# A Strassen product done by the same scheme once more inside: one of seven products in the second input phase

## The chip, the core and the metric

The kernel runs on one core of a Trainium2 chip. The metric is device time: 910.96 us is the median of 3 runs of the kernel before (910.4 to 911.87). One execution was profiled; its trace gives every instruction of TensorE (PE, with its weight loads as PEld), VectorE (DVE), ScalarE (ACT), GpSimd (POOL) and SyncE (SP), and every DMA.

## What is computed

The reference is one layer of a pooling mixer on x (1 x 4096 x 1024, float32):

```
normed = rms_norm(x, norm_w)
u, gate = split(normed @ in_w, 2)            # in_w: 1024 x 2048
pooled = trailing means of u over 2/4/8/16 frames (4 channel groups) - u
mixed  = pooled (group by group) @ group_w + group_b
y      = mixed * scale * silu(gate)
out    = rms_norm(x + y @ out_w, final_norm_w)
```

## The kernel before

The kernel is three phases of matrix products, in float32. Every operand is cut into a high part that TensorE takes exactly and a low part with the rest (`split`, lines 167 to 170: ScalarE copies the high part, L165, VectorE subtracts to get the low part, L159), and a product is three matmuls: high-high, high-low, low-high (`mm3`, L603).

Phase "a" works on half of the channels, phase "b" on the other half; both take 4 blocks of 1024 frames. Phase "o" is the output projection, 8 blocks of 512 frames. A block of any phase is a product of 2 x 2 quarters, done by the scheme of Strassen and Winograd: 7 products P1 to P7 instead of 8, on sums of quarters. On the side of the frames the sums are S1 = A21 + A22, S2 = S1 - A11, S3 = A11 - A21, S4 = A12 - S2 in their usual names. In the input phases the order is P1, P2, P7, P6, P5, P4, P3; P3 is S4 times the weight quarter B22. One product is one step of the loop over `steps` (lines 1069 to 1071), so there are 28 + 28 + 56 steps.

A step of the input phases is 48 matmuls of 512 columns (`product_in`, line 609). P1 and P2 accumulate in PSUM banks 0 to 3; ScalarE copies P1's result to banks 4 to 7 as well, where P6, P5 and P3 are added on; P7 and P4 accumulate in banks 0 to 3. `evict_in` (line 806) takes the results out: ScalarE copies those of P1, P2, P6, P7 and P3, VectorE adds those of P5 and P4 onto earlier ones (L156). So while P3 runs in banks 4 to 7, banks 0 to 3 hold nothing that is still to be accumulated.

Operands come through 11 + 8 buffers of 128 x 1024 (`st` and `vt`, a queue by age: the one free the longest is taken). In phase a, `form_in` (line 547) normalizes the quarters of x and makes the sums; the operands of P1, P2, P7 and P4 are stored to DRAM by GpSimd's queue (`split_halves`, line 509), and phase b loads these four (`load_saved`, line 528) and makes S2 (for P6), S1 (for P5) and S4 (for P3) again with six subtractions and additions per block on VectorE. Four operand tiles (`op`) are used in turn.

Beside the products VectorE has the pooling of every half block: `pool` (line 745) is a chain of shifted additions on 128 x 1024, then L783 and L788, and a store to DRAM (`yd`). It is put off by some steps after P4 and P3 (`pool_later`, line 1116). In the last block of phase b the weights of phase o are loaded and split (`load_w`), one product's weights after each step.

Phase o has steps of 24 matmuls of 512 columns (`product_out`, line 716). Its order is P1, P7, P6, P2, P5, P4, P3, and VectorE adds each result onto x (`evict_o`, L1033). P6, P5 and P3 accumulate one after the other in the same pair of banks, so P3 can start there only when P5's result has been added out. In its blocks 2 to 7, P2 is already done by the same scheme once more inside (`product_inner`, L701, 42 matmuls of 256 columns in place of 24 of 512; `add_inner`, L711).

The framework orders each engine's instructions when the kernel is built, by the order in which they are written and `issue_after` marks; on the chip every queue is worked off in that order.

```
    def pool_later(n):
        kind, b, i = steps[n]
        if i == P4:
            args = (b, 0 if kind == "a" else 1, 1, ev.pop("22"), ev.pop("21"))
            wait = int(b == 0) if kind == "a" else 1 if b < NB - 1 else 2
```

## Time and profile before

| what | value |
|---|---|
| median of 3 runs | 910.96 us |
| profiled execution: its own time, its span | 911.84 us, 909.7 us |
| PE busy, PEld busy | 900.6 us (99%), 790.1 us (87%) |
| DVE busy, ACT busy, POOL busy | 764.5 us (84%), 461.8 us (51%), 49.9 us (5%) |
| phase b in the trace | 324.59 to 614.89 us |
| phase o in the trace | from 614.89 us |

PE's busy time says that PE is never without work in the middle of the kernel; what the reader needs beside it is how far the other engines are ahead of PE at each step. That is seen in tables by step (a step of phase b is 10.37 us, one of phase o 5.18 us) and in the timeline of one engine. In the timeline an instruction is shown with its full duration, while the next of the same engine starts a little before its end; the distance of the starts is what a full queue pays. A timeline's columns are start, duration (of all where there are several), engine, line, operation, tiles, shapes, and in brackets the idle time before it.

### The profile page before, as it was taken

Reading aid. Unit: us, or ns where it says so; the run is one execution under the profiler, and the core shown is the slowest. Engines: PE = TensorE matmul, PEld = TensorE weight load, DVE = VectorE, ACT = ScalarE, POOL = GpSimd, SP = SyncE. Lnnn points to the kernel's source line nnn. Section 1 sums busy time; section 2 is a strip of 40 time slices with the busy share of each in tenths; the row PEclk is TensorE's granted clock in tenths of the full one; section 3 lists DMA queues with packets and bytes.
Section 4 is the critical chain, followed back from the end, with each engine's and each line's share of the span. In section 5 each row is a group of like instructions: output and inputs, shape, how many; then the busy total and the mean of one; then the engine's idle time right before and its main releaser. Section 6 shows DMA issues by size and latency. Waiting matters only on the chain.

```text
span 909.7 us, 11455 instructions
## 1 busy us (share of the span) xinstructions
PE 900.6 (99%) x4320; PEld 790.1 (87%) x4320; DVE 764.5 (84%) x909; ACT 461.8 (51%) x693; POOL 49.9 (5%) x124
## 2 busy tenths in 40 slices
PE   9999999999999999999999999999999999999997
PEld 7888888888888888888888888888888898888886
DVE  3889995985995997696798699699989878978886
ACT  7869547547446565355445545644424424335334
POOL 0020100100110000000000000000201001001000
PEclk9999999999999999999999999999999999999998
DMA  9977766577675454116616714636385464464332
GB/s 341 401 291 240 276 235 230 189 270 253 217 272 196 156 202 145 47 64 212 255 47 234 275 70 158 235 105 219 137 280 181 149 226 155 146 232 139 116 139 93
DMA packets 66807, 178.08 MB, mean 196 GB/s; under 512 B 6080, under 2 KB 23872, under 8 KB 66752
## 3 DMA queue, kind: packets, MB, share of 16 engines
q1 hardware_dynamic: 60176, 155.83, 48.8%
q0 software_dynamic: 5856, 20.46, 6.1%
q10 hardware_dynamic: 720, 1.06, 0.3%
q8 instruction: 34, 0.56, 0.2%
q14 instruction: 21, 0.17, 0.1%
HBM read 116.50 MB, written 60.83 MB: 195 GB/s over the span
## 4 chain that ended last, share of the span: by engine, by line
PE 91%; DMA 4%; DVE 3%; issue 1%; ACT 0%; SPq 0%; POOL 0%; DVEq 0%; ACTq 0%; POOLq 0%
PE bank L603 88%; PE bank L701 3%; DMA early<-in_wut 2%; DMA st<-in_x 1%; DMA vt<-yd 1%; DVE vt L1033 1%; PE bank L406 1%; DVE op L159 1%; DVE st L159 0%; DVE vt L916 0%; ACT st L943 0%; DVE vt L162 0%; DVE vt L711 0%; SPq L370 0%; DVE st L1033 0%
## 5 line engine op out<-in xcount | busy, mean ns | idle before, releaser
L603 PE MATMUL bank<-op,w 128*128 128x512 f32 x2688 | 580.9, 379 | 0.0
L603 PEld LDWEIGHTS bank<-op,w 128*128 128x128 f32 x2688 | 508.5, 189 | 71.8 <-ACT bank L165 0.4
L603 PE MATMUL bank<-w,op 128*128 128x512 f32 (+1 forms) x1212 | 262.2, 377 | 0.0
L603 PEld LDWEIGHTS bank<-w,op 128*128 128x128 f32 x1212 | 226.3, 189 | 30.7
L165 ACT ACTIVATE op<-st 128x1024 fp32r<-128x1024 f32 x129 | 134.7, 1053 | 142.2 <-PE bank L603 90.5
L159 DVE TENSOR_TENSOR op<-st,op 128x1024 fp32r<-128x1024 f32 x129 | 156.8, 1222 | 51.7 <-ACT op L165 51.3
L156 DVE TENSOR_TENSOR vt<-vt 128x1024 f32<-128x1024 f32 (+6 forms) x72 | 88.2, 1236 | 0.6
L159 DVE TENSOR_TENSOR op<-vt,op 128x1024 fp32r<-128x1024 f32 x43 | 52.5, 1222 | 19.8 <-ACT op L165 19.6
L165 ACT ACTIVATE vt<-bank 128x512 f32<-128x512 f32 x82 | 47.6, 593 | 41.4 <-PE bank L603 40.5
L165 ACT ACTIVATE op<-vt 128x1024 fp32r<-128x1024 f32 x43 | 45.1, 1053 | 39.3 <-PE bank L603 30.2
L159 DVE TENSOR_TENSOR st<-st,st 128x1024 f32<-128x1024 f32 (+1 forms) x43 | 47.0, 1111 | 2.3 <-ACT st L912 1.3
L165 ACT ACTIVATE bank<-bank 128x512 f32<-128x512 f32 x48 | 27.9, 581 | 32.9 <-PE bank L603 32.9
L1033 DVE TENSOR_TENSOR vt<-bank,vt 128x512 f32<-128x512 f32 (+1 forms) x55 | 37.1, 677 | 7.4 <-PE bank L603 7.0
L165 ACT ACTIVATE st<-bank 128x512 f32<-128x512 f32 x48 | 27.8, 593 | 28.7 <-PE bank L603 22.3
L207 POOL TENSOR_SCALAR oms<-oss 128x2 f32<-128x2 f32 x14 | 8.4, 601 | 565.5 <-ACT st L912 460.6
L159 DVE TENSOR_TENSOR w<-st,w 128x1024 fp32r<-128x1024 f32 x25 | 30.2, 1223 | 7.8 <-ACT w L165 7.8
L165 ACT ACTIVATE w<-st 128x1024 fp32r<-128x1024 f32 x25 | 26.0, 1052 | 14.2 <-PE bank L603 9.6
L788 DVE SCALAR_TENSOR_TENSOR st<-vt,colt,st 128x512 f32<-128x512 f32 x46 | 32.7, 752 | 0.1
L1033 DVE TENSOR_TENSOR st<-bank,st 128x512 f32<-128x512 f32 x42 | 28.8, 692 | 3.9 <-PE bank L603 3.7
L783 DVE SCALAR_TENSOR_TENSOR vt<-vt,vt 128x1024 f32<-128x1024 f32 x24 | 29.4, 1227 | 0.3
L916 DVE SCALAR_TENSOR_TENSOR vt<-vt,ors,st 128x1024 f32<-128x1024 f32 x18 | 22.5, 1282 | 7.9 <-POOL ors L225 7.9
L165 ACT ACTIVATE st<-st 128x1024 f32<-128x1024 f32 x16 | 16.9, 1059 | 21.8 <-DVE st L156 21.7
(132 smaller groups left out, 619.0 us busy)
## 6 DMA issues: line engine op xcount, KB each, us to landing
st<-in_x SPq DMA_DIRECT2D x30, 512.0 KB, 5.3
st<-in_xt SPq DMA_DIRECT2D x28, 512.0 KB, 5.6
sd<-st POOLq DMA_DIRECT2D x28, 512.0 KB, 4.6
vt<-in_x SPq DMA_DIRECT2D x27, 512.0 KB, 4.5
st<-sd SPq DMA_DIRECT2D x24, 512.0 KB, 4.2
yd<-st SPq DMA_DIRECT2D x23, 512.0 KB, 2.6
st<-yd SPq DMA_DIRECT2D x20, 512.0 KB, 4.6
out<-vt SPq DMA_DIRECT2D x18, 512.0 KB, 3.6
```

The source lines that it names most:

```text
L156: nc.vector.tensor_tensor(out=dst, in0=a, in1=b, op=ALU.add)
L159: return nc.vector.tensor_tensor(out=dst, in0=a, in1=b, op=ALU.subtract)
L165: return nc.scalar.activation(dst, src, func)
L207: (nc.vector if on_vector and not first else nc.gpsimd).tensor_scalar(out=ms, in0=ss, scalar1=1.0 / D, scalar2=EPS, op0=ALU.mult, op1=ALU.add)
L406: latest[0] = nc.tensor.matmul(ps, a[:, kk, 2 * j + t, :], maps, start=t + m == 0, stop=t == 1 and m == len(pairs) - 1,).ins
L603: latest[0] = nc.tensor.matmul(ps, a, b, start=start and n == 0, stop=stop and n == 2, skip_group_check=True).ins
L701: latest[0] = nc.tensor.matmul(ps, x1, x2, start=i in (P1, P7) and k + n == 0, stop=k == 1 and n == 2, skip_group_check=True,).ins
L783: nc.vector.scalar_tensor_tensor(out=s[:, :, at : at + H], in0=s[:, :, at : at + H], scalar=1.0 / win, in1=v[:, :, HIST:], op0=ALU.mult, o ...
L788: nc.vector.scalar_tensor_tensor(out=sg[:, j], in0=s[:, j, at : at + H], scalar=bias_c[2 * grp + j], in1=sg[:, j], op0=ALU.add, op1=ALU.mult,)
L916: nc.vector.scalar_tensor_tensor(out=us[j], in0=us[j], scalar=rs[:, j : j + 1], in1=fw[0], op0=ALU.mult, op1=ALU.mult,)
L1033: partial["added"] = nc.vector.tensor_tensor(out=dst, in0=src, in1=dst, op=ALU.add).ins
```

## The change

P3 of each block of phase b (S4 times B22) is done by the scheme of seven once more: quarters of the quarter, 7 products of 12 matmuls of 256 columns (84 in place of 48 of 512). The inner P2, P4 and P3 add straight into banks 4 to 7; the inner P1 and, by copies of it, P6 and P5, and P7, use banks 0 to 3, from where VectorE adds them onto the rows (`to_rows`). The inner sums of the weight are made once, in block 0 (`form_inner_in`), and kept in four of the `st` buffers, which are lent until the end of phase b. The inner sums of S4 are made in each block (`split_inner_in`) and split into two operand tiles (`split_sums`).

Phase a now stores the operands of all seven products, and phase b loads all seven instead of making S2, S1 and S4. Loads of phase b are issued 2 steps ahead instead of 3 (but for the first three of block 0), some of phase o's first block 2 or 3 instead of 4. The pooling of P4's half in blocks 0 to 2 of phase b is put off by two steps instead of one. `make_wo` comes one step earlier. The buffers that phase o keeps for its own inner product are set aside from block 0 on.

```diff
@@ sd (operands that are stored)
-            for i in (P1, P2, P7, P4)
+            for i in ORDER_IN
@@ load_in, form_in, split_in
+        if q:
+            s[i] = load_saved(b, i)
...
+        if q:
+            t = split_halves(s[i])
+            if i == P3:
+                t = split_inner_in(t, s[i])
+            for u in s.pop(i):
+                give(u)
+            return t
@@ new functions
+    def split_inner_in(ts, us):
+        (a11, a21), (a12, a22) = ([quarter(u, g) for g in range(2)] for u in us)
+        vs = [take("p (n k s a) -> p n k s a", n=2, k=2, s=2) for _ in range(2)]
+        (s4, s2), (s3, s1) = ([v[:, n] for n in range(2)] for v in vs)
+        sub(s3, a11, a21)
+        sub(s2, a22, s3)
+        sub(s4, a12, s2)
+        add(s1, s2, a11)
...
+    def split_sums(t, n):
+        v, products = t["sums"][n]
+        o = next_op("p (x n k s a) -> p x n k s a", x=2, n=2, k=2, s=2)
+        split(o, v)
...
+    def inner_in(t, sets, then):
+        y, (one, six, seven, five) = sets["y"], sets["v"]
...
+        def to_rows(bank, *places):
+            src = bank.rearrange("p (c a s) -> p c s a", c=2, s=2)
+            for g, n in places:
+                dst = rows[n][:, :, HIST:].rearrange("p c (s a) -> p c s a", s=2)
+                dst = dst[:, :, :, g * P : (g + 1) * P]
+                add(dst, src, dst)
+        go(P2)
+        go(P1)
+        copy(six, one)
+        go(P4)
+        for c in range(2):
+            from_y(c)
+        to_rows(one, (0, 0))
+        go(P3)
+        then()
+        go(P6)
+        copy(five, six)
+        for c in range(2, 4):
+            evicted[0] = from_y(c).ins
+        to_rows(six, (1, 0))
+        go(P7)
+        to_rows(seven, (1, 0), (1, 1))
+        go(P5)
+        to_rows(five, (0, 1), (1, 1))
@@ pool_later
-            wait = int(b == 0) if kind == "a" else 1 if b < NB - 1 else 2
+            wait = int(b == 0) if kind == "a" else 2
@@ load_reach
-        return 4 if kind == "o" else 3
+        if kind == "o":
+            return 2 if (b, i) == (0, P1) else 3 if b == 0 and i in (P7, P6, P2) else 4
+        return 2 if kind == "b" and (b or i not in (P1, P2, P7)) else 3
@@ main loop
-        if kind == "o" and b == 1 and len(kept) < 4 and not inner_w:
+        if kind == "o" and b < 2 and not inner_w and (b or i in (P5, P4, P3)):
...
-        advance("split", n, split_step, split_reach)
+        due = lambda: advance("split", n, split_step, split_reach)
+        inside = kind == "b" and i == P3
+        if inside:
+            for half in range(2):
+                split_sums(split_up[n], half)
+        else:
+            due()
+        if kind == "b" and b == 0 and i in in_stages:
+            with tc.issue_after(latest_split[0]), tc.issue_after(latest_copy[0]):
+                form_inner_in(in_stages.index(i))
...
-        run(n)
+        run(n, behind=due if inside else None)
+        if kind == "b" and b == NB - 1 and i == P3:
+            st.end()
...
-            if kind == "b" and b in (1, 2) and i == P5:
+            if kind == "b" and b in (1, 2) and i == P6:
                 make_wo(b - 1)
```

More of the change, by code (lines that the diff above doesn't have):

```diff
@@ L56, in keep, with lend, end @@
         return self.renew(self.free.popleft()[1])
+    def lend(self):
+        t = self.free.popleft()[1]
+        self.lent.append(self.index_of(t))
+        return self.renew(t)
+    def end(self):
+        for i in self.lent:
+            Slots.clock += 1
+            self.free.append((Slots.clock, self.revert(i)))
     def give(self, ap):
@@ L119, with index_of, revert @@
     st = Slots(sts)
+    def index_of(t):
+        return next(i for i, u in enumerate(sts) if u is t)
     def renew(t):
-        i = next(i for i, u in enumerate(sts) if u is t)
-        return mem.tile([P, D], F32R, tag=f"st{i}", name=f"inner{i}")
-    st.renew = renew
+        return mem.tile([P, D], F32R, tag=f"st{index_of(t)}", name=f"inner{index_of(t)}")
+    def revert(i):
+        sts[i] = mem.tile([P, D], F32, tag=f"st{i}", name=f"st{i}")
+        return sts[i]
+    st.index_of, st.renew, st.revert = index_of, renew, revert
     vt = Slots(
@@ new lines, in split_inner_in @@
+    def split_inner_in(ts, us):
[6 more added lines that the diff above has]
+        add(s1, s2, a11)
+        t = {
+            P1: [quarter(ts[0][:, x], 0) for x in range(2)],
+            P2: [quarter(ts[1][:, x], 0) for x in range(2)],
+            P4: [quarter(ts[1][:, x], 1) for x in range(2)],
+        }
+        t["sums"] = ((vs[0], (P3, P6)), (vs[1], (P7, P5)))
+        return t
```

112 lines of the change are left out of this document (82 added, 30 removed).

## The prediction

> **What bounds the kernel now.** I read the page's busy times first, then PE's waits, then PE's timeline for the rates, then tables by step around the places that the change touches, and at the end VectorE's timeline there. The page:
>
> ```profile
> PE 900.6 (99%) x4320; PEld 790.1 (87%) x4320; DVE 764.5 (84%) x909; ACT 461.8 (51%) x693; POOL 49.9 (5%) x124
> PE 91%; DMA 4%; DVE 3%; issue 1%; ACT 0%; SPq 0%; POOL 0%; DVEq 0%; ACTq 0%; POOLq 0%
> ```
>
> PE's waits in the whole kernel:
>
> ```profile
> PE bank L406 <- DMA early<-in_wut: 1.0, 3, 0.4
> PE bank L1135 <- PEq L1433: 0.8, 1, 0.8
> PE bank L406 <- DMA early<-in_group_w: 0.4, 1, 0.4
> PE bank L701 <- DVE vt L711: 0.3, 1, 0.3
> ```
>
> After the start PE waits once, for 0.3 us. So matmuls that go away are worth their full time, and each wait that comes in costs its full time. PE's timeline gives the rates:
>
> ```profile
> 47.41 567.64 PE L603 MATMUL bank<-op,w 128*128 128x512 f32 x2628
> 614.89 88.22 PE L603 MATMUL bank<-w,op 128*128 128x512 f32 x408
> 702.95 1.50 PE L701 MATMUL bank<-w,op 128*128 128x256 f32 x12
> 706.29 2.75 PE L603 MATMUL bank<-w,op 128*128 128x512 f32 x12
> ```
>
> A matmul of 512 columns takes 567.5 / 2628 = 0.216 us; the 30 of 256 columns between 702.95 and 706.29 take 0.111 each. Phase b ends at 614.89, which I call O; a step is 10.37 us before O and 5.18 after it.
>
> How far VectorE is ahead at that border is told by the steps of the end of phase b and the start of phase o (columns: window, its length, then busy time of PE, PEld, DVE, ACT, POOL, clock, DMA share, GB/s):
>
> ```profile
> 542.30:614.89 72.59, 72.59 (x339) 63.62 (x338) 64.17 (x63) 39.92 (x55) 0.00 (x0) 1.00 0.49 167
> 583.79:594.15 10.36, 10.36 (x49) 9.08 (x48) 6.54 (x8) 4.95 (x7) 0.00 (x0) 1.00 0.62 204
> 594.15:604.52 10.37, 10.37 (x49) 9.08 (x48) 10.37 (x12) 4.83 (x7) 0.00 (x0) 1.00 0.15 51
> 604.52:614.89 10.37, 10.37 (x50) 9.08 (x49) 10.37 (x12) 6.36 (x8) 0.00 (x0) 1.00 0.45 151
> 614.89:625.26 10.37, 10.37 (x50) 9.09 (x49) 10.37 (x12) 5.53 (x9) 0.00 (x0) 1.00 0.61 205
> 625.26:635.63 10.37, 10.37 (x50) 9.09 (x49) 10.37 (x13) 2.08 (x2) 0.00 (x0) 1.00 0.63 212
> 635.63:646.00 10.37, 10.37 (x50) 9.09 (x49) 10.37 (x13) 1.06 (x1) 0.00 (x0) 1.00 0.23 91
> ```
>
> The whole last block leaves VectorE 8.4 us idle, but from 594 to 646 it has no idle time at all: it is working off a queue, and PE is only just not waiting. How much spare that is, its timeline says:
>
> ```profile
> 567.64 2.36 DVE L159 TENSOR_TENSOR op<-st,op 128x1024 fp32r<-128x1024 f32 x2
> 590.06 1.23 DVE L159 TENSOR_TENSOR w<-st,w 128x1024 fp32r<-128x1024 f32 x1 [2.52 <-ACT w L165]
> 591.20 0.68 DVE L156 TENSOR_TENSOR vt<-bank,vt 128x512 f32<-128x512 f32 x1
> 592.93 1.28 DVE L156 TENSOR_TENSOR vt<-bank,vt 128x512 f32<-128x512 f32 x2
> 640.99 1.43 DVE L788 SCALAR_TENSOR_TENSOR vt<-vt,colt,vt 128x512 f32<-128x512 f32 x2
> 643.45 0.71 DVE L1033 TENSOR_TENSOR st<-bank,st 128x512 f32<-128x512 f32 x1
> ```
>
> At full queue (distance of starts) an operation on 128 x 1024 costs 1.14 us, one on 128 x 512 0.60, an L788 0.66. The row at 591.20 adds out the first bank of P5 in the last block; the row at 643.45 adds out the first bank of P5 in phase o's first block. Phase o's P3 accumulates in that bank next and is due six steps after O, at 614.89 + 31.1 = 646.0. The add ends at 643.45 + 0.71 = 644.16: 1.8 us spare. This is the tightest place near the change.
>
> **The change, part by part.**
>
> PE: 84 matmuls for 48 gives 48 x 0.216 - 84 x 0.111 = 10.37 - 9.35 = 1.02 us per block, 4.1 us in all. This is the whole gain, all of it before O. TensorE's operands have the same kind of strides as in L701, so I keep 0.111.
>
> VectorE, per block: six operations go (S2, S1, S4 on two halves, 6 x 1.14 = 6.8 us), in the steps of P7, P6 and P5. Into P3's step come four sums of S4's quarters (4 x 0.60), two low parts (2 x 1.14) and six adds from banks 0 to 3 (6 x 0.60): 8.3 us. Net 1.5 us, small, but moved from steps with room to the step of P3. The weight's inner sums, once in block 0, are 4 x 0.60 + 2 x 1.14 = 4.7 us, in the steps of P7, P6 and P5, which have room as P5's shows:
>
> ```profile
> 366.06:376.43 10.37, 10.37 (x50) 9.09 (x49) 4.91 (x6) 3.06 (x5) 0.00 (x0) 1.00 0.18 60
> ```
>
> ScalarE gets two more splits (about 2 us) and two bank copies (1.2 us) per block. It is 50% busy in phase b, but in P3's step the copy of inner P1 to P6's bank and of P6 to P5's stand in line between splits: inner P5 starts 8.0 us after P3's start, and the copies, each half of the 1.06 us of a 128 x 1024, end about then. From 0 to 0.3 us per block; I take 0.
>
> Pooling: P4's half moves from P3's step to the next block's P1. One half is 7 shifted additions, 2 L783 and 4 L788: 9 x 1.14 + 4 x 0.66 = 13 us. In blocks 0 to 2 this only moves. But the last block, which had one half left over from block 2, now has two, while its own two still go to phase o. So the last block gets 13 + 1.5 us more on VectorE and had 8.4 idle.
>
> The queue at the border. As the changed kernel is built, VectorE's list between the same two adds (P5's first bank in the last block, P5's first bank in phase o) holds all that it held before and in addition six adds of 128 x 512 from the inner banks, three of the sums, two operand splits and one L783: 9 x 0.60 + 3 x 1.14 = 8.8 us. The stretch took 644.16 - 591.20 = 53.0 and will take 61.7. The room: the first add can't start before P5's first bank is done, which is three groups of six matmuls before P5's end (3.9 us), then P4 10.37, P3 9.35, six steps of phase o 31.1: 54.7 us. So PE must wait 61.7 - 54.7 = 7.0 us in phase o, at P3 or in pieces before it. To this comes a late start. The first half of P5's new weights is loaded into a buffer that the second half of P6's frees:
>
> ```profile
> 588.97 1.06 ACT L165 ACTIVATE w<-st 128x1024 fp32r<-128x1024 f32 x1 [2.69 <-PE bank L603]
> ```
>
> ```profile
> st<-wod SPq DMA_DIRECT2D x15, 512.0 KB, 4.2
> ```
>
> P6's weights are free at P6's end, 30.1 us before O (P5, P4, and P3 at 9.35); copy 1.06, low part 1.14, load 4.2, copy 1.06, low part 1.14 make 8.6, and the list has that low part right before the first add: it starts at O - 21.5 and not at O - 23.6, 2.1 us late. The loads' wait stands on SyncE's queue, where the first loads of phase o are behind it; they have over 10 us. Together 9.1 us.
>
> After the wait. From that add to the operand split that P7 of the next block needs, the list holds 11.2 us (five of 128 x 512, two L788, six of 128 x 1024, one tiny); PE has P3 and P1 in between, 10.4 us. Another 0.8 us, unless PE is slow here, since the wait is long. What the clock does in such a wait the trace shows at its end:
>
> ```profile
> 902.00:903.00 1.00, 1.00 (x10) 0.82 (x8) 0.72 (x5) 1.00 (x4) 0.00 (x0) 1.00 0.40 154
> 904.00:905.00 1.00, 0.00 (x0) 0.00 (x0) 0.85 (x4) 0.63 (x3) 0.00 (x0) 1.00 0.55 213
> 905.00:906.00 1.00, 0.00 (x0) 0.00 (x0) 0.93 (x4) 0.66 (x1) 0.00 (x0) 0.55 1.00 383
> ```
>
> ```profile
> 0.78 3.45 PE L1135 MATMUL bank<-const-bfloat16-1.0 128*128 128x512 bf16 x8 [0.78 <-PEq L1433]
> ```
>
> The clock is halved 2 us after the last matmul, and the eight matmuls at the very start ran at 0.43 us each, twice the 0.216. I take 3.45 us at half speed after the wait: 1.7 us, with which PE arrives after the split, so that the 0.8 is inside it. [...]
>
> Stores and loads: 24 stores of 512 KB more on GpSimd's queue in phase a, 24 loads more on SyncE's in phase b, 12.6 MB each way.
>
> ```profile
> 34.30:324.59 290.29, 290.29 (x1349) 254.34 (x1348) 245.97 (x291) 174.09 (x270) 26.21 (x49) 1.00 0.68 241
> 324.59:614.89 290.30, 290.30 (x1347) 254.49 (x1346) 243.16 (x244) 143.50 (x206) 0.00 (x0) 1.00 0.45 158
> ```
>
> ```profile
> sd<-st POOLq DMA_DIRECT2D x28, 512.0 KB, 4.6
> st<-sd SPq DMA_DIRECT2D x24, 512.0 KB, 4.2
> ```
>
> That is 43 GB/s more on 241 and 158. A load issued two steps ahead has 20.7 us for 4.2, so the loads are covered. The stores hold their buffers 4.6 us longer; most are taken again steps later. One place is tight: in phase a's first block the changed list puts P6's results into the buffers that P5's operands leave, after their store.
>
> ```profile
> 64.69 2.36 DVE L156 TENSOR_TENSOR st<-early,st 128x1024 f32<-128x1024 f32 x2
> 74.48 0.57 ACT L165 ACTIVATE st<-bank 128x512 f32<-128x512 f32 x1
> ```
>
> ```profile
> 75.76:86.13 10.37, 10.37 (x50) 9.09 (x49) 8.87 (x14) 10.36 (x16) 0.54 (x1) 1.00 0.68 207
> ```
>
> ```profile
> wvd<-early POOLq DMA_DIRECT2D x4, 512.0 KB, 7.5
> ```
>
> These operands are ready at 65.9 and 67.0 and P6's first result is copied out at 74.48, with ScalarE full behind it. A store that lands as fast as most (4.6) is done at 71.6, one as slow as the stores of that time (7.5) at 74.5, and one that has to wait for three issues of about a us more at 77.5. From 0 to 3 us; I take 0.
>
> Sum, against the profiled execution's own 911.84: 911.84 - 4.1 + 9.1 + 1.7 = 918.5. The median of the runs is 0.88 below that execution, so **917.7 us**.
>
> **The rivals.**
>
> 1. *VectorE takes the load and PE never waits* (faster): then only the 4.1 us is left, 906.9. For it: VectorE is 84% busy, and the last block has 8.4 us idle. Against it: the idle time lies before the first of the two adds, and the overrun is after it. It is faster only if the stretch grows by less than about 5 us instead of 8.8 (spare 1.8, less 1.0 for the shorter P3, plus the 4.1).
> 2. *The bound alone*: the loads of weights come sooner, so the late start doesn't happen, and the clock holds; 911.84 - 4.1 + 7.0 - 0.88 = 913.9.
> 3. *The clock holds*, because the wait comes in several short pieces: 0.8 in place of 1.7, 916.8. For it: P6's split is behind the same queue, so part of the wait comes there. Against it: the last add of P5 has the largest delay. [...]
> 4. *Stores hold up phase a as well*: the 3 us above on top of the forecast, 920.7. The first block's last steps would show PE waiting for ScalarE's copies out of banks 4 to 7.
> 5. *No change that can be measured*: the scheme does its work and PE waits about the 4.1 us that it saves, because part of the 8.8 us stands in VectorE's idle times; 911.
>
> **How the numbers follow.** Forecast 0.42, rival 1 0.09, rival 2 0.16, rival 3 0.17, rival 4 0.10, rival 5 0.06. A measurement of this kernel can tell about 0.2%, 1.8 us. Slower: 0.42 + 0.16 + 0.17 + 0.10 = 0.85; same 0.06; faster 0.09. The range leaves out rivals 1 and 5 and goes from a little under rival 2 to over rival 4: 912.8 to 921.5.
>
> **What would show it.** P3's steps in phase b at 9.35 us with the 256-column rate of 0.111; PE gapless through phase b; VectorE without idle from P5 of the last block until phase o's second block; PE waits of 7 to 9 us on VectorE's add of P5's result in phase o's first block, some of it a step or two earlier at P6; the granted clock at 0.5 there; no further PE waits after the second block. It is wrong if VectorE's adds from the inner banks or its list are shorter than counted, if PE waits already inside P3's steps, or if the first block of phase a shows waits.

## The result and the profile after

The changed kernel takes 933.31 us (median of 6 runs, 931.7 to 935.44), the kernel before 911.53 (6 runs on the same chip, 910.4 to 912.41): a ratio of 1.0241, 95% interval 1.023 to 1.0252, so 2.4% slower. The prediction was slower, 917.7 with a range up to 921.5. The sign was right; the time missed by 15.6 us.

The profiled execution of the changed kernel is its slowest, 935.44 us with a span of 933.5. Its page, and PE's waits in the whole kernel:

```profile
PE 904.6 (97%) x4464; PEld 793.8 (85%) x4464; DVE 776.1 (83%) x939; ACT 473.4 (51%) x711; POOL 56.5 (6%) x148
PE 61%; DVE 18%; DMA 11%; ACT 5%; issue 4%; POOL 1%; SPq 0%; DVEq 0%; ACTq 0%; POOLq 0%
```

```profile
PE bank L628 <- DVE st L1171: 6.0, 1, 6.0
PE bank L628 <- ACT st L183: 5.5, 3, 3.7
PE bank L709 <- ACT bank L183: 5.1, 5, 1.4
PE bank L628 <- DVE op L177: 2.3, 2, 1.4
PE bank L839 <- DVE st L849: 1.3, 1, 1.3
```

Before, PE waited 0.3 us after the start. Now results of ScalarE and of VectorE are late, in five kinds of places. (Of the changed kernel's lines, L183 is `copy` on ScalarE, L177 and L174 `sub` and `add` on VectorE, L628 the matmul of 512 columns, L709 that of the new inner product, L1171 the adds of phase o's results, L839 and L849 phase o's inner product and its adds.) PE's timeline says where they lie:

```profile
77.64 1.56 PE L628 MATMUL bank<-op,w 128*128 128x512 f32 x6 [1.27 <-ACT st L183]
...
227.46 12.85 PE L628 MATMUL bank<-op,w 128*128 128x512 f32 x45 [3.71 <-ACT st L183]
...
477.65 1.60 PE L709 MATMUL bank<-op,inner 128*128 128x256 f32 x12 [1.40 <-ACT bank L183]
...
625.48 1.60 PE L709 MATMUL bank<-op,inner 128*128 128x256 f32 x12 [0.91 <-ACT bank L183]
...
639.27 21.47 PE L628 MATMUL bank<-w,op 128*128 128x512 f32 x98 [1.40 <-DVE op L177]
...
666.78 12.29 PE L628 MATMUL bank<-w,op 128*128 128x512 f32 x48 [6.04 <-DVE st L1171]
680.00 20.34 PE L628 MATMUL bank<-w,op 128*128 128x512 f32 x93 [0.93 <-DVE op L177]
...
733.30 0.94 PE L839 MATMUL bank<-inner,op 128*128 128x256 f32 x6 [1.33 <-DVE st L849]
```

All kernels here have the same phases, so the clearest account is the time from the first matmul of a phase to the first of the next (of phase o to its last matmul). It comes from the start times of the matmuls in each profiled execution; before it is about 291, 290 and 288 us for phases a, b and o. The table gives the differences to that, of all kernels that ran, with the medians of their runs (the kernel before beside them: 911.53 for the changed kernel, 910.9 to 911.2 for the others):

| kernel | phase a | phase b | phase o | median us | ratio, 95% interval |
|---|---|---|---|---|---|
| changed kernel | +9.2 | +2.8 | +11.8 | 933.31 | 1.023 to 1.0252 |
| e3_stores | +7.9 | 0.0 | -0.4 | 918.43 | 1.0066 to 1.0096 |
| e22_behind | +7.6 | 0.0 | +0.3 | 918.53 | 1.0065 to 1.0095 |
| e23_both | +4.7 | +1.0 | -0.3 | 915.59 | 1.0028 to 1.0056 |
| e6_t3_later | +4.1 | +3.7 | +12.9 | 932.6 | 1.0219 to 1.0259 |
| e7_plain | +8.9 | +0.9 | +6.4 | 924.97 | 1.0125 to 1.0169 |
| e9_plain_kept | +8.9 | +1.5 | +2.0 | 921.78 | 1.0102 to 1.0132 |
| e16_plain_keep | +8.5 | +1.1 | +2.1 | 923.09 | 1.012 to 1.0147 |
| e2_last_plain | +8.0 | +2.8 | +4.5 | 925.56 | 1.0145 to 1.0176 |
| e8_norm_later | +9.0 | +2.1 | +4.4 | 926.62 | 1.015 to 1.018 |
| e10_last_kept | +9.0 | +2.0 | +4.7 | 925.84 | 1.0119 to 1.0172 |
| e13_last_copy | +8.2 | +2.8 | +2.5 | 924.98 | 1.0133 to 1.0166 |
| e17_last_keep | +7.9 | +2.7 | +1.0 | 921.81 | 1.0104 to 1.0144 |
| e1_pool | +9.1 | +3.5 | +12.9 | 933.71 | 1.0223 to 1.0261 |
| e5_no_copies | +7.9 | +3.5 | +12.9 | 934.37 | 1.0235 to 1.0268 |
| e11_copy_first | +7.6 | +3.4 | +12.7 | 933.34 | 1.0227 to 1.026 |
| e18_keep | +7.4 | +2.2 | +10.1 | 932.58 | 1.022 to 1.0264 |
| e4_formed | +0.4 | +18.1 | +14.4 | 941.89 | 1.0323 to 1.0354 |
| e21_one | 0.0 | -1.0 | -0.2 | 910.66 | 0.9986 to 1.0004 |

The prediction in this form is 0, -4.1 and +10.8. So the miss lies in phase a (9.2 us) and phase b (6.9). Phase o is 1.0 us off in sum, but not part by part, as the section on the prediction says.

### The profile page after: what moved, and what is told of

It reads as the page before. It is cut to its first block, busy times and chain, and to the rows that moved or that the text cites. A ratio compares the mean times of both kernels' runs of the same rounds, so it can differ in the third digit from the quotient of the medians.

```text
span 933.5 us, 11935 instructions
## 1 busy us (share of the span) xinstructions
PE 904.6 (97%) x4464; PEld 793.8 (85%) x4464; DVE 776.1 (83%) x939; ACT 473.4 (51%) x711; POOL 56.5 (6%) x148
## 4 chain that ended last, share of the span: by engine, by line
PE 61%; DVE 18%; DMA 11%; ACT 5%; issue 4%; POOL 1%; SPq 0%; DVEq 0%; ACTq 0%; POOLq 0%
PE bank L628 57%; DVE vt L174 5%; DVE op L177 4%; PE bank L839 3%; DMA early<-in_wut 2%; DMA st<-wvd 2%; DMA st<-wod 1%; DVE st L177 1%; DMA st<-sd 1%; DMA wvd<-early 1%; DMA st<-in_x 1%; PE bank L709 1%; DVE vt L177 1%; ACT op L183 1%; DVE st L174 1%
## 5 line engine op out<-in xcount | busy, mean ns | idle before, releaser
L628 PE MATMUL bank<-op,w 128*128 128x512 f32 x2496 | 543.7, 381 | 5.5 <-ACT st L183 5.5
L628 PEld LDWEIGHTS bank<-op,w 128*128 128x128 f32 x2496 | 473.2, 190 | 74.4 <-ACT st L183 6.7
L628 PE MATMUL bank<-w,op 128*128 128x512 f32 (+1 forms) x1212 | 264.8, 379 | 8.4 <-DVE st L1171 6.0
L628 PEld LDWEIGHTS bank<-w,op 128*128 128x128 f32 x1212 | 226.9, 190 | 40.9 <-issue 6.4
L183 ACT ACTIVATE op<-st 128x1024 fp32r<-128x1024 f32 x127 | 132.3, 1052 | 106.6 <-PE bank L628 69.5
L177 DVE TENSOR_TENSOR op<-st,op 128x1024 fp32r<-128x1024 f32 x127 | 153.8, 1220 | 31.8 <-ACT op L183 31.3
L183 ACT ACTIVATE op<-vt 128x1024 fp32r<-128x1024 f32 x53 | 55.7, 1054 | 79.3 <-PE bank L628 39.0
L174 DVE TENSOR_TENSOR vt<-vt 128x1028 f32<-128x1028 f32 (+6 forms) x72 | 86.9, 1232 | 0.4
L177 DVE TENSOR_TENSOR op<-vt,op 128x1024 fp32r<-128x1024 f32 x53 | 64.6, 1219 | 25.3 <-ACT op L183 25.3
L183 ACT ACTIVATE vt<-bank 128x512 f32<-128x512 f32 x88 | 50.2, 593 | 31.8 <-PE bank L628 31.7
L183 ACT ACTIVATE bank<-bank 128x512 f32<-128x512 f32 x56 | 32.7, 584 | 36.0 <-PE bank L628 35.8
L1171 DVE TENSOR_TENSOR vt<-bank,vt 128x512 f32<-128x512 f32 (+1 forms) x57 | 38.4, 676 | 6.3 <-PE bank L628 6.1
L183 ACT ACTIVATE st<-bank 128x512 f32<-128x512 f32 x42 | 23.8, 594 | 37.2 <-PE bank L628 21.6
L174 DVE TENSOR_TENSOR vt<-bank,vt 128x512 f32<-128x512 f32 (+1 forms) x63 | 40.6, 679 | 1.0 <-ACT bank L183 0.5
L177 DVE TENSOR_TENSOR st<-st,st 128x1024 f32<-128x1024 f32 (+2 forms) x29 | 30.7, 1074 | 12.3 <-DMA st<-wvd 8.6
L177 DVE TENSOR_TENSOR w<-st,w 128x1024 fp32r<-128x1024 f32 x25 | 29.9, 1218 | 8.1 <-ACT w L183 8.1
L1171 DVE TENSOR_TENSOR st<-bank,st 128x512 f32<-128x512 f32 x40 | 27.2, 686 | 7.2 <-PE bank L628 7.0
L183 ACT ACTIVATE w<-st 128x1024 fp32r<-128x1024 f32 x25 | 25.9, 1053 | 10.7 <-DMA st<-wod 8.0
L535 POOL DMA_DIRECT2D sd<-st x42 | 22.5, 537 | 132.5 <-DVE tmp L180 40.4
L709 PE MATMUL bank<-op,inner 128*128 128x256 f32 x192 | 23.8, 278 | 5.1 <-ACT bank L183 5.1
```

The source lines that it names most:

```text
L174: nc.vector.tensor_tensor(out=dst, in0=a, in1=b, op=ALU.add)
L177: return nc.vector.tensor_tensor(out=dst, in0=a, in1=b, op=ALU.subtract)
L183: return nc.scalar.activation(dst, src, func)
L535: first_saves.append(nc.gpsimd.dma_start(out=saved[h], in_=u).ins)
L628: latest[0] = nc.tensor.matmul(ps, a, b, start=start and n == 0, stop=stop and n == 2, skip_group_check=True).ins
L709: latest[0] = nc.tensor.matmul(ps, x1, x2, start=i in (P1, P7) and ct + k + n == 0, stop=k == 1 and n == 2, skip_group_check=True,).ins
```

## Experiments on phase a: the stores

**e3_stores**: the kernel before, with all seven sums stored and nothing else.

```
-            for i in (P1, P2, P7, P4)
+            for i in ORDER_IN
```

> The kernel before with one change: all seven operand sums of each block are stored in phase a, so 24 stores of 512 KB come in; nothing is loaded that was not loaded, nothing else is touched. Theory (the stores collide with other transfers of phase a): PE waits for ScalarE's copies out of banks 4 to 7 in the first block (about 2.3 us) and, in the third block, where a difference of two weight quarters is made from loads (line 313 of the changed kernel), 3.7 us and the halved clock after it (2.9 us): 909.7 + 9 = about 919 for the span, some 920.5 for the time. Rival (the stores alone are covered, and the two places come from another part of the change): 911.5, no change. If only the first block's buffers matter: 914.

It takes 918.43 us, 7.4 more, where 9 were expected, and has PE's waits of the changed kernel in the same two places (from start to start of the matmuls 1.1 and 0.7 us more at 75 to 78 us, 4.2 at 222), none elsewhere. The stores alone make most of phase a's loss, 7.9 of 9.2 us in the profiled executions. Most of the rest I put down to the halved clock after the second wait: in the changed kernel it is 0.50 for 5.8 us from the first matmul after that wait on (227.46 to 233.2), which costs 2.9 us, and in e3_stores the 7.9 less these waits leaves 1.9 for it, an estimate. How they do it shows in the third block, where `save_t3` loads four weight quarters and makes two differences. DMA and engines in that step, before and in the changed kernel (columns as in the prediction's tables):

```profile
199.31:209.68 10.37, 10.37 (x50) 9.09 (x49) 7.03 (x7) 7.30 (x11) 0.00 (x0) 1.00 0.61 191
```

```profile
201.20:211.50 10.30, 10.30 (x49) 9.02 (x48) 6.81 (x6) 7.08 (x12) 2.14 (x4) 1.00 1.01 362
```

The DMA engines go from 61% to full. The four loads of `save_t3` (L295 before, L313 after), minimum, median and maximum from issue to landing:

```profile
DMA to landing us min/median/max: 3.6/4.1/4.6
```

```profile
DMA to landing us min/median/max: 5.0/7.4/9.8
```

The loads are links of a chain: load, difference, store, load into the buffer that this frees, second difference, and then ScalarE can copy P6's result into the buffers that the differences held. Before, the two differences started at 208.88 and 218.75, and ScalarE came out of the chain just in time:

```profile
208.88 1.22 DVE L159 TENSOR_TENSOR st<-st,st 128x1024 f32<-128x1024 f32 x1
...
218.75 1.23 DVE L159 TENSOR_TENSOR st<-st,st 128x1024 f32<-128x1024 f32 x1 [0.20 <-DMA st<-wvd]
```

```profile
220.05 2.07 ACT L165 ACTIVATE st<-bank 128x512 f32<-128x512 f32 x4 [2.77 <-DVE st L159]
```

Now the second difference waits for its load, the copy for the difference, and P5's matmuls for the copy:

```profile
215.66 1.23 DVE L177 TENSOR_TENSOR st<-st,st 128x1024 f32<-128x1024 f32 x1 [4.31 <-DMA st<-wvd]
...
225.50 1.23 DVE L177 TENSOR_TENSOR st<-st,st 128x1024 f32<-128x1024 f32 x1 [4.25 <-DMA st<-wvd]
```

```profile
226.81 2.06 ACT L183 ACTIVATE st<-bank 128x512 f32<-128x512 f32 x4 [7.14 <-DVE st L177]
```

From the first load's issue (202.3 before, 204.7 now) to the first difference it is 10.9 us now and was 6.5: 4.4 longer, since the slowest of the four loads, 9.8 us, is one of the two that this difference needs. From there to the second difference it is 9.8 us now and was 9.9, so the load in between costs nothing more. ScalarE had stood idle 2.77 us for that buffer before and stands 7.14 now, 4.4 longer as well. Before, the copy began at 220.05 and P5's step at 220.9, so the chain had less than a us to spare; now PE waits 3.71, and its clock is 0.50 from 226.4 to 233.2.

**e22_behind** and **e23_both** take up the first block. There the trace has another link than the prediction's: S2's two stores wait for VectorE at the head of GpSimd's queue (3.57 and 0.72 us of idle time before them), two stores of weights stand behind them, and ScalarE's copy into the weights' buffer waits for these. ScalarE's timeline in the changed kernel, with P6's first copy-out 2.5 us later than before (74.48):

```profile
71.89 1.06 ACT L183 ACTIVATE w<-early 128x1024 fp32r<-128x1024 f32 x1 [2.42 <-DMA wvd<-early]
...
77.02 0.58 ACT L183 ACTIVATE st<-bank 128x512 f32<-128x512 f32 x1
```

e22_behind puts S2's stores behind the weights' (on top of e3_stores); e23_both also makes `save_t3` a step later.

```
-        later = q == 0 and b == 0 and i in (P1, P2)
+        later = q == 0 and b == 0 and i in (P1, P2, P6)
# e23_both, too:
-        if kind == "a" and b == 2 and i == P7:
+        if kind == "a" and b == 2 and i == P6:
```

> The run with the stores alone (the kernel before, all seven sums stored), but in the first block S2's two stores stand behind the stores of weights on GpSimd's queue and not ahead of them. Theory (S2's stores wait for VectorE, the weights' stores stand behind them in order and land late, ScalarE's copy into the weights' buffer waits 2.4 us for that, and the copies out of P6's banks stand behind it): PE's waits of 1.1 and 0.7 us at 75 to 78 go; the one at 222 stays: 918.4 less 1.8 to 2.2, about 916.4. Rival (P6's results wait for a buffer that is still being stored, as the prediction had it, or for the traffic as a whole): the two waits stay, 918.

> The same, and in addition the difference of two weight quarters a step later (P6 of block 2), as in the run with that edit on the changed kernel. Theory (these are the two places where the stores cost): 911.2 and up to 1.5 more for what that edit left at 254 to 330 us in the changed kernel: 911 to 913. Rival (what is taken away in one place comes back in the next steps of phase a): 914 to 917.

In e22_behind the copy into the weights' buffer does not wait any more, and in its place the copy-out does, for the buffer that S1's store holds, as the prediction had bounded it:

```profile
75.41 0.60 ACT L165 ACTIVATE st<-bank 128x512 f32<-128x512 f32 x1 [1.50 <-DMA sd<-st]
```

The two waits fall from 1.8 us in e3_stores to 1.25, and the time does not change (918.53, the rival's 918 and not the theory's 916.4). Both links end within a us of each other; taking one away leaves the other. e23_both is 3 us better than the stores alone, and 4.6 above the kernel before: the wait at 222 is gone, and waits of 1.75, 1.27 and 0.9 us stand at 254, 266 and 329 us in its place. The theory's 911 to 913 was wrong here, the rival right.

**e6_t3_later** makes that last edit alone in the changed kernel.

> The changed kernel, but the difference of two weight quarters (lines 307 to 318: four loads, two subtractions, two stores) is made in block 2's step of P6 and not of P7, one step later. Theory (its loads collide with four stores of sums that are issued within 3 us before them, land in 7.4 us and not 4.1, and the buffers that the difference holds come back too late for P6's results): with the loads away from these stores PE's wait of 3.7 us and the halved clock after it go, 5.6 to 6.6 less: 927 to 928. Rival (the difference holds buffers wherever it stands while stores are under way): the wait moves a step or two later and stays, 931 to 935.

Median 932.6, 0.7 below the changed kernel and within its spread. The theory's 927 to 928 missed. Phase a is 5.1 us shorter in the profiled execution, of which 0.9 and 1.1 come back in phases b and o; the wait at 224 is gone, and shorter ones stand at 255, 267 and 329 us. So the long wait hangs on where these loads stand, and a place for them that costs nothing was not found. The edit moves the whole chain and not the landing alone; that the slow landing makes the wait rests on the chain's times above.

## Experiments on phase o: the border

**e2_last_plain** and **e1_pool** part two explanations of the wait at phase o's P3: the longer list on VectorE, or the second half of the pooling in the last block.

```
# e2_last_plain
-            if i == P3:
+            if i == P3 and b < NB - 1:
                 t = split_inner_in(t, s[i])
# e1_pool
-            wait = int(b == 0) if kind == "a" else 2
+            wait = int(b == 0) if kind == "a" else 1 if b < NB - 1 else 2
```

> The changed kernel, but the last block's P3 in phase b is a plain product of 48 matmuls, as in the kernel before; blocks 0 to 2 keep the scheme. Theory (VectorE's queue between the two adds of P5's first bank decides): that list falls from 61.0 to 52.3 us, which it was before, so PE's waits at P3 of phase b's last block (1.7), at the second and sixth step of phase o (1.4 and 6.0), the halved clock (1.7) and the wait after it (0.9) go: 11.7 less and 1.0 more for the plain product, 922 to 924. Rival (the load of the last block as a whole, with two halves of the pooling in it, or the late start of the weights decides): the waits at the border shrink by 2 to 5 us only, 929 to 932.

> The changed kernel, but P4's half of the pooling stands where it stood before (one step after P4 in blocks 0 to 2), so the last block of phase b has one half less of it, 13 us of VectorE. Theory (the list between the two adds decides): that list is 59.9 instead of 61.0 us, so PE's waits at the border shrink by about 1 us, while the pooling back in P3's step may cost ScalarE's bank copies 0 to 2 us: 931 to 935. Rival (the second half of the pooling overloads the last block): the border's 11.7 us go, 921 to 924.

e1_pool takes 13 us of VectorE out of the last block and changes nothing (933.71; the wait at P3 is 6.8 us). In e2_last_plain the two adds of the prediction (P5's first bank in the last block and in phase o's first) start 52.3 us apart and not 62.3, and the waits at phase o's third step and at its P3 are gone (the second and the sixth in the expectation, which counts from 0). Phase o falls from +11.8 to +4.5. The time, 925.56, lies between the theory's 922 to 924 and the rival's 929 to 932, since one wait of 3.07 us is left, with which phase o still loses 4.5:

```profile
670.92 1.35 PE L628 MATMUL bank<-w,op 128*128 128x512 f32 x4 [3.07 <-DVE op L177]
```

**e7_plain**, the changed kernel with a plain P3 in all blocks, has that wait too (4.1 us at 666), so it is not the scheme's. It takes 924.97, the rival's 921 or more and not the theory's 918 to 919. Its VectorE timeline there (L1050 is the norm's product):

> The changed kernel without its inner scheme: all seven sums are stored and loaded, and P3 of phase b is a plain product of 48 matmuls in all four blocks. Theory (stores cost phase a 7.4 us; the loads cost nothing; without the scheme VectorE has 6.8 us less in each block than before, the list between the two adds is 48.5 us, and PE waits nowhere from phase b on): 911.0 + 7.4, 918 to 919, with no wait of PE after 230 us. Rival (loads of sums two steps ahead, or the moved half of the pooling, cost something by themselves in phase b or at the border): 921 or more.

```profile
662.88 1.23 DVE L177 TENSOR_TENSOR st<-vt,vt 128x1024 f32<-128x1024 f32 x1 [2.52 <-issue]
...
666.82 2.48 DVE L1050 SCALAR_TENSOR_TENSOR st<-st,ors,st 128x1024 f32<-128x1024 f32 x2 [0.92 <-POOL ors L243]
669.22 1.22 DVE L177 TENSOR_TENSOR op<-st,op 128x1024 fp32r<-128x1024 f32 x1
```

The first row makes S3 for P7 of phase o's second block. In the built list its target is the buffer whose pooled result went off to DRAM at 658.59; it starts 4.3 us later, after 2.52 us in which VectorE stands idle. That it waits there for this store to land is my reading; stores from `st` to `yd` take 3.6 us in the median of the changed kernel. Then a final norm's chain (square, root, reciprocal, two products) stands in the list, and only behind it the split that P7 waits for. In the kernel before, S3 went to another buffer and did not wait, and the split stood ahead of the norm's products. Three runs look for the edit that did this.

**e8_norm_later** calls that norm a step later (with the last block plain). **e9_plain_kept** (all plain) and **e10_last_kept** (last block plain) undo one edit of the diff, which sets four buffers aside already in phase o's first block:

```
# e8_norm_later, in evict_o
-        elif not final and i in (P4, P3):
+        elif b and not final and i in (P4, P3):
             finish(b, 1 if i == P4 else 0)
+        elif not b and i == P3:
+            with tc.issue_after(latest_split[0]):
+                finish(b, 1)
+            finish(b, 0)
# e9_plain_kept, e10_last_kept
-        if kind == "o" and b < 2 and not inner_w and (b or i in (P5, P4, P3)):
+        if kind == "o" and b == 1 and not inner_w:
```

> As the run with a plain P3 in the last block, and in addition the first half of phase o's first final norm (called at line 1240 in P4's step) is called a step later, behind the split of P7's operand, so that this split stands ahead of the norm's two products in VectorE's list. Theory (what was left of the border's wait, 3.2 us and the halved clock after it, is VectorE waiting in order for the norm's square, root and reciprocal with that split behind): 925.6 less 5, 920 to 921. Rival (the split is late because VectorE has more to do, not because it waits): 1.7 us less at most (its two idle times there), 924.

> As the run with a plain P3 in all four blocks, and in addition the four buffers for phase o's inner weights are set aside when they were before (in phase o's block 1 and not already from P5 of block 0). Theory (with four buffers fewer at the border, the sum for P7's operand is written to the buffer whose pooled result is just being stored, and has to wait 2.5 us for that store to land, with the final norm's chain ahead of the split; with the buffers free the sum gets one that has long been idle): PE's wait of 4.2 us and the halved clock after it go, 925.0 less 6, 918 to 919.5, which is the kernel before plus the stores' 7.4. Rival (the wait comes from the later loads or the moved pooling): 924 to 926.

> As the run with a plain P3 in the last block, and in addition the four buffers for phase o's inner weights are set aside when they were before. Theory (as in the run with plain P3 and this edit, and nothing else is late): PE's wait of 3.2 us at P7 of phase o's second block and the halved clock after it go, 925.6 less 5 to 6, 919.5 to 920.5. Rival (VectorE is behind after the border in any case, as the run with the norm a step later showed, where the wait moved to phase o's third block): the wait moves to 710 to 740 us and stays, 924 to 927.

The wait at 666 to 670 is gone in all three, so either change takes it away, the norm's place in the list or the buffers. But in all three a wait of 2.5 us comes in at 716 to 718, in phase o's third block, behind the next norm (e9_plain_kept 921.78, e8_norm_later 926.62, e10_last_kept 925.84), and no theory's time was met (e10_last_kept fell within its rival's). **e16_plain_keep** (all plain), **e17_last_keep** (last block plain) and **e18_keep** (scheme in all blocks) undo a second edit besides, the number of spare buffers in phase o:

```
-        elif kind == "o" and b:
+        elif kept:
             keep[0] = 0
```

> The changed kernel with a plain P3 in all blocks, with the four buffers set aside as before, and in addition the spare of three vt buffers is dropped in phase o only while buffers are set aside (as before) and not in every block from 1 on. Theory (the way in which buffers are shared out orders VectorE's list so that operand splits stand behind the norm's chain; with both edits undone they do not): the wait of 2.5 us at 715.7 goes, 921.8 less 2.6, 919 (the kernel before plus the stores' 7.4). Rival (the moved pooling or the loads): 921 to 922.

> The changed kernel with a plain P3 in the last block alone, and both edits of the buffers undone. Theory (with the last block plain the list between the two adds is as before, and with the buffers as before nothing else is late after phase b): no wait of PE after 600 us, 925.8 less 5 to 6, 919.5 to 920.5; what stays above the kernel before is the stores (7.4) and the waits in P3's steps (3.9) less 3.05. Rival (VectorE's total work at the border): a wait of 2 to 4 us stays after 640 us, 923 to 926.

> The changed kernel with both edits of the buffers undone and the inner scheme in all four blocks. Theory (the list between the two adds, 61 against 52 us, makes the wait of 6 us at phase o's P3 and the halved clock, the buffers make the small waits after it): the wait at P3 stays, those after it (0.9 and 1.3) go: 933.3 less 2.2, 931. Rival (the buffers make the large wait too): under 927.

Now PE's waits in e17_last_keep, and in e18_keep:

```profile
PE bank L628 <- ACT st L183: 5.4, 3, 4.0
PE bank L709 <- ACT bank L183: 4.4, 4, 1.4
...
PE bank L839 <- DVE vt L849: 0.8, 1, 0.8
```

```profile
PE bank L628 <- DVE st L1171: 6.0, 1, 6.0
...
PE bank L628 <- DVE op L177: 1.5, 1, 1.5
...
PE bank L839 <- DVE vt L849: 0.8, 1, 0.8
```

With the last block plain and the buffers as before, phase o loses 1.0 us; with the scheme in the last block it loses 10.1, and the wait of 6.0 at P3 is there as in the changed kernel. So of phase o's 11.8 us the list makes 9.1 (e18_keep less e17_last_keep) or 7.3 (the changed kernel less e2_last_plain), and the buffers 1.7 (the changed kernel less e18_keep) or 3.5 (e2_last_plain less e17_last_keep), since the two causes overlap. e18_keep, at 932.58, is near its theory's 931; e17_last_keep, at 921.81, has lost the large waits after 600 us, and lies above its theory's 919.5 to 920.5 since its phase b is +2.7. The small rest of 1.0 us (waits of 0.8 to 0.9 at the inner products) was not followed: e16_plain_keep, where 919 was expected, has two of them and takes 923.09, which is no better than e9_plain_kept.

## Experiments on phase b: the inner products

In P3's steps PE waits for the copies from bank to bank. ScalarE's timeline in block 1 shows why they are late: the line is full from 471.7 to 478.6, and the copy of P6's bank (476.97) stands behind two splits of the next product and four copies out.

```profile
471.69 1.07 ACT L183 ACTIVATE st<-st 128x1024 f32<-128x1024 f32 x1 [1.12 <-DVE st L174]
472.66 0.59 ACT L183 ACTIVATE bank<-bank 128x512 f32<-128x512 f32 x1
473.17 1.05 ACT L183 ACTIVATE op<-st 128x1024 fp32r<-128x1024 f32 x1
474.11 1.08 ACT L183 ACTIVATE vt<-bank 128x512 f32<-128x512 f32 x2
475.07 1.07 ACT L183 ACTIVATE op<-st 128x1024 fp32r<-128x1024 f32 x1
476.02 1.09 ACT L183 ACTIVATE vt<-bank 128x512 f32<-128x512 f32 x2
476.97 0.63 ACT L183 ACTIVATE bank<-bank 128x512 f32<-128x512 f32 x1
477.49 1.08 ACT L183 ACTIVATE op<-vt 128x1024 fp32r<-128x1024 f32 x1
```

**e5_no_copies** leaves the two copies out (its sums lack P1 in P6's bank and P6 in P5's); **e11_copy_first** puts the second ahead; **e13_last_copy** has that order, a plain last block and the buffers set aside later.

```
# e5_no_copies
-        copy(six, one)
-        copy(five, six)
-                            ps, x1, x2, start=i in (P1, P7) and ct + k + n == 0,
+                            ps, x1, x2, start=i in (P1, P7, P6, P5) and ct + k + n == 0,
# e11_copy_first
-        then()
         go(P6)
-        copy(five, six)
-        for c in range(2, 4):
-            evicted[0] = from_y(c).ins
+        with tc.issue_after(copy(five, six).ins):
+            for c in range(2, 4):
+                evicted[0] = from_y(c).ins
+            then()
```

> The changed kernel without the two copies from bank to bank in each inner P3: inner P6 and P5 start their banks afresh, so the sums of P1 with P6 and of P6 with P5 are left out of the result. Theory (the copies stand in ScalarE's line behind splits and copies out, and PE waits for them; in the last block that wait is part of the border's and comes back there): PE's waits in P3's steps go in blocks 1 and 2, 3.4 to 4.3 us less, 929 to 930. Rival a (the waits are those of the banks that the copies read, not of the copies): no change, 933. Rival b (all five waits count in full): 6 us less, 927.

> The changed kernel, but in inner_in the copy of P6's bank to P5's is put ahead of the copies out of banks 6 and 7 and of the next step's splits on ScalarE. Theory (ScalarE's order alone makes this copy 2 us late, PE waits 1.4 us for it in blocks 1 and 2): these two waits go and no other takes their place; the last block's comes back at the border: 933.3 less 2.8, 930 to 931. Rival (the splits, now later, make the next block's P1 wait, or VectorE is behind there anyway): 932.5 to 935.

> Three of the edits together: plain P3 in the last block, the buffers set aside later, and the copy from P6's bank ahead in ScalarE's line. If each names its wait rightly, only the stores' 7.4 us and the first copy's wait (0.6 to 0.8 in blocks 1 and 2) are left beside the three blocks' gain of 3.05: 911.2 + 7.4 - 3.05 + 1.4 = 917. Rival (the waits are of VectorE's total work and move on when one is taken away): 922 to 926.

e5_no_copies takes 934.37, and the theory's 929 to 930 missed. The waits for copies are gone, in block 1 without any other in their place; in block 2's P3 step PE waits 1.4 us for VectorE's add, and in the last block there are others.

```profile
540.08 1.60 PE L709 MATMUL bank<-op,w 128*128 128x256 f32 x12 [1.41 <-DVE st L174]
```

e11_copy_first takes 933.34: no wait for the second copy, but 0.5 to 0.6 at the next block's P1 and 0.85 later, for the splits and copies that now come after. e13_last_copy, at 924.98, missed its 917, in part in the same way (phase b is +2.8) and in part by the wait of 2.6 us at 717 (phase o is +2.5). My theory, ScalarE's order alone, fell. What the runs show is that a wait taken away in P3's steps comes back as others, for ScalarE or for VectorE, in the same step or later ones. That neither line has the time there, whichever order it has, fits this, but no run shows it by itself. Nor is all of phase b's loss the scheme's: with a plain P3 in all blocks (e7_plain, e9_plain_kept, e16_plain_keep) it is still 0.9 to 1.5 us, mostly in waits for ScalarE at 429 and 501.

**e4_formed** takes the added stores and loads away: the sums are formed again in phase b, as before, and the scheme stays in all blocks. **e21_one** is the kernel before with the scheme in block 0 of phase b alone.

```
# e4_formed: load_in, form_in and split_in of the kernel before, with split_inner_in at P3
# e21_one: the same, and
+        if q and i == P3 and b in INNER:       # INNER = (0,)
+            t = split_inner_in(t, s[key])
# pool_later, load_reach, make_wo's step and the buffers of phase o as in the kernel before
```

> The changed kernel without its stores and loads: S2, S1 and S4 are formed again in phase b, as in the kernel before; the inner scheme stays in all four blocks. Theory (stores cost phase a what the run with the stores alone showed; the queue between the two adds, 57.7 us here and 61.0 in the changed kernel, decides at the border): 7.4 less and about 3.4 less, 922 to 924. Rival (VectorE, which forms the sums again, 6.8 us a block, comes later to all of P3's operands and adds): the waits in P3's steps grow by what the stores gave back, 928 to 935.

> The kernel before with the inner scheme in block 0 of phase b alone: the sums are formed again and not stored, the pooling, the reaches of loads and the buffers are as before, the weight's inner sums are formed in block 0. Theory (the scheme is worth 1.02 us of PE in a block where VectorE and ScalarE are in time, and block 0 has 12 us of idle VectorE): 910.0 to 910.5 where the kernel before has 911.2. Rival (its six adds and two splits stand in the block that follows and PE waits for them): 912 or more.

e4_formed takes 941.89, the slowest of all. Phase a is as before, but phase b loses 18.1 us, 9.0 of them in one wait for ScalarE's copy-out at 567: with the sums formed again, there is no room for the scheme (whether VectorE's work or the buffers decide there was not tried apart). Theory (922 to 924) and rival (928 to 935) were both too low. In e21_one phase b is 0.98 us shorter and PE waits nowhere behind the start. That is the scheme's gain, in a block with room. The time, 910.66 against 911.03 in 11 and 15 runs, is too near to be told from the kernel before; no kernel here is measurably faster than it.

## Why the prediction was wrong

Point by point, in the prediction's own terms:

- *PE's gain, 1.02 us a block, 4.1 in all*: right. e21_one has 0.98 for one block, and the rate of 0.111 us held.
- *VectorE's queue at the border, 9.1 us at phase o's P3*: right in place and mechanism. The add of P5's first bank in the last block starts at 603.66 and that of phase o's ends at 666.63: 63.0 us, where 61.7 were predicted. PE waits 6.0 at P3, 1.4 at the third step, and 1.7 already in the last block's P3, there for the copies: 9.1. The late start was there too (the first add 2.6 us after the bank was done, where 2.1 were taken). That the sum agrees to the digit, with both of its parts larger, is partly luck. e2_last_plain and e18_keep show that this list makes it, e1_pool that the half of the pooling in the last block doesn't.
- *After the wait 0.8 us, inside the slow clock's 1.7*: wrong in part. The clock was slow for 3.4 us after the wait (0.50 from 666.78 to 670.1), so its loss came as predicted, by luck: behind the shorter wait of 3.71 us in phase a it was slow for 5.8. But waits of 0.9 at 680 and 1.3 at 733 came on top. They make up for the 1.7 us of the border's wait that fell into phase b, and so phase o's sum came out near the 10.8. For the wait at 680 the prediction had counted the list's work as it stood, and not VectorE's idle time in it: 0.5 us for ScalarE's square in the norm and 0.6 for GpSimd's part of its factor in the changed kernel, and in e7_plain 2.5, put down to a store. That the diff takes four buffers away at the border and changes the spare was in the diff and not priced.
- *The stores: from 0 to 3 us in the first block, I take 0; the rest hidden*: this step failed most, 9.2 us in the profiled execution, 7.4 in e3_stores. In the first block 2.1 us fell inside the bound, by two links of nearly the same length, one of which the prediction had. In the third block nothing had been bounded: "most are taken again steps later" looked at the buffers of the stored sums, and not at other transfers on the same path. Before, the DMA engines were 0.61 busy in `save_t3`'s step; four stores there make it full, and the first two loads of a chain with less than a us to spare landed in up to 9.8 us where the slowest of all had taken 4.6. PE's wait of 3.7 us and the halved clock behind it are the price. The spare and the 0.61 were in the trace before, and so was a landing in a full step: the 7.5 us that the prediction quotes for four stores are of 54 to 57 us, and from 55.0 to 65.4 us the DMA engines were full (1.01). So the price could have been worked out.
- *The copies in P3's steps, 0 to 0.3 us a block*: wrong, 6.1 us in the six waits of blocks 1 to 3 from start to start of the matmuls, of which the last block's 2.0 belong to the border's 9.1. The prediction compared the copies with the time of PE's P5 and took ScalarE's 50% as room; in the step itself its line is full for 7 us. But the copies are only the wait that ends last in block 2: e5_no_copies shows VectorE's add behind them there. Why the time does not fall when they go stays open.
- *The rivals*: rival 4 (stores hold up phase a) is the one that came, at three times its price and mostly in a place that it did not name; 0.10 was too little for it. Two of the signs that the prediction had named for itself being wrong came: waits inside P3's steps, and waits in the first block of phase a.

## What to carry to other kernels

When transfers are added, look in each step's DMA share for a chain of load, compute and store whose result frees a buffer, and price that chain with a slower landing (here up to 9.8 us for 4.6, with the DMA share at 1.01 for 0.61). Matmuls saved on a full TensorE were worth their time here only in a step where the other engines' in-order lines had room (0.98 us in e21_one's block 0, against 6.1 us of waits in these steps of the changed kernel's blocks 1 to 3): look at that step's line and not at the average of the phase. Where buffers are tight, an edit to who holds them reorders whole lists, so compare the built order of the engine that is nearest to its limit, and count the waits inside it beside the work.

## What was not expected of the hardware

How long the clock was slow did not go by the length of the wait. In the changed kernel the granted clock is 0.50 for 6.8 us at the wait of 3.71 us (226.4 to 233.2, 5.8 us of it after the wait) and for 6.8 us at the wait of 6.04 (663.4 to 670.2, 3.4 us of it after the wait). And one length of wait came with a slow clock in one kernel and without it in another: PE waits 2.57 us at 717 in e8_norm_later and in e13_last_copy, and the two kernels go on like this (PE's busy time and count, clock, DMA share, GB/s; first e8_norm_later, then e13_last_copy):

```profile
720.10:723.40 3.30, 3.30 (x8) 0.50 0.49 149
```

```profile
720.10:723.40 3.30, 3.30 (x19) 1.00 0.45 144
```

Eight matmuls in one and 19 in the other in the same 3.3 us. The twelve matmuls of 512 columns behind the wait take 4.51 us in the first and 2.83 in the second, so after the same wait PE lost 1.7 us more or nothing. What decides between the two was not shown by any run, and so such a wait could not be priced from its length. The kernels with such waits spread by up to 5.9 us from run to run (e10_last_kept, 921.33 to 927.19) where the kernel before spreads by 1.9; this may be a part of that.
